# Block 0's products at every third mark, the last gather spread to twelve columns from the end, block 6's outputs divided between the last two phases

## The chip, the core and the metric

The kernel runs on one core of one Trainium2 chip. The metric is the device time of one execution in microseconds (us). Five engines work side by side, each in its own fixed order of instructions: PE (TensorE, matmuls; PEld is its weight load), DVE (VectorE), ACT (ScalarE), POOL (GpSimd, which here issues the gathers) and SP (SyncE, which issues the other transfers). An engine whose next instruction waits lets nothing behind it pass.

## The reference, cut to what matters

Of the 1024 tokens, each picks 8 times 16 experts out of 16384; an expert is one row of 1024 numbers in `u_tab` and one in `v_tab`.

```
def block(xb):                    # 128 tokens
    ...
    idx = jnp.take_along_axis(cand_i, best_pos, axis=-1)      # 128 experts a token
    gate = jax.nn.softmax(best_s, axis=-1)
    u = u_tab[idx]
    v = v_tab[idx]
    act = jax.nn.gelu(jnp.einsum('td,thkd->thk', xb, u).astype(jnp.float32))
    return jnp.einsum('thk,thkd->td', (gate * act).astype(xb.dtype), v)
```

A mixer (norm, pooling, gated part, output projection) stands before this and a norm behind it. The change touches neither.

## The kernel before

The 1024 tokens are eight blocks of 128. The mixer and the scores go over the first 256 tokens, then the middle 512, then the last 256. The expert part is done in two ways.

**Dense, blocks 2 to 5** (the middle 512 tokens). `gates_dense` builds a table of gates with one-hot matmuls (L591, `mm<-oh` and `mu<-oh`, 128 groups of four tokens). Then `dense` goes over 128 columns of 128 experts each: it loads `raw_u` and `raw_v` (512 KB each), splits both into high and low parts (`uh` on ACT, `ul` on DVE, likewise `v`), makes 24 matmuls into `mu`, applies gelu on ACT (L666, `a<-mu`, once a column, so its starts tell where the columns are), multiplies by the gates (L667) and splits the result into `wh` and `wl`. After every third column 72 matmuls into `mm` follow, with eight additions into `hD` on DVE (L645).

**Sparse, blocks 0, 1, 6 and 7.** POOL gathers rows of the tables, one gather for a position j of 128, each 128 rows of 4 KB (512 KB). "U of a block" is 128 gathers from `peer_u`, each followed by one multiply-and-sum on DVE (`sparse_u`, L505, `junk`). "V of a block" follows when its U is whole. For blocks 0, 1 and 6 (`sparse_v`) it is 32 steps; a step is four gathers from `peer_v` and sixteen `po` matmuls on PE (L538). For block 7, the one named by `SUMMED`, it is 128 gathers and 128 multiply-adds on DVE instead, each needing the one before it (`sparse_s`, L559).

The rows land in two sets of buffers: `rowt` with 8 and `rowv` with 4. A gather waits until its buffer's last reader is done. `sparse(phases)` takes phases in turn. `EARLY` runs beside the gates and uses `rowt` alone. `LATE` runs beside the columns. In a phase that has both U and V, U takes `rowv` and V takes `rowt`; in a phase that has one kind alone, gathers go to the two sets by turns, twelve buffers in all. V of block 7 counts as V.

Two things set where a sparse instruction stands. The program's text emits dense columns and sparse steps by turns, at an even pace (the loop at the end of `hybrid_block`), and the framework's scheduler then lays out every engine's order with a clock of its own: of what is ready on that clock it takes what the text has first. A gather that has a free buffer may so come long before its place in the text. `marks` are matmuls of the mixer and gate stage in the order of the text; `anchors` with `BEHIND` say after which mark a step of block 0's V may stand (`behind`, `issue_after`): step j not before mark 4 + 4j.

Of the kernel before, what the change touches and what calls it, by code (L numbers as in the profile page):

```python
# [27 lines left out]
NK = 128  # L28
# [14 lines left out]
GROUP = 3  # L43
# [2 lines left out]
GI = 4  # L46
OH = 3

BEHIND = (4, 4)

TURN = 6

# [1 line left out]
QUAD = 4  # L54

EARLY = ({"U0": 128}, {"U1": 16}, {"V0": 128, "U1": 48})
LATE = ({"U1": 64}, {"V1": 128, "U6": 128}, {"V6": 128, "U7": 128}, {"V7": 128})

SUMMED = 7

RUNS = ((0, 1, 16), (1, 7, 8), (8, 8, 1))
NC = sum(na * nb for _, na, nb in RUNS)
# [3 lines left out]
def hybrid_block(ctx: ExitStack, tc: tile.TileContext, t: dict, out: bass.AP):  # L66
# [399 lines left out]
    def turn(b):  # L466

        d, srcs = picked.pop(b)
        p = ps.tile([P, HALF], F32, name="mm")[:, :P * len(srcs)]
        for i, src in enumerate(srcs):  # L470
            nc.tensor.transpose(p[:, i * P:(i + 1) * P], src, ident)
        nc.vector.tensor_copy(d, p.rearrange("p (i j) -> p i j", j=P))
        turned[b] = d
# [2 lines left out]

    homes = {"U": [(gat, "rowt", ROWS)], "V": [(gat, "rowt", ROWS)]}

    def gather(table, ids, turn):

        home = homes["U" if table == "peer_u" else "V"]
        pool, name, bufs = home[turn % len(home)]
        rowt = pool.tile([P, D], F32, name=name, bufs=bufs)
        ins = nc.gpsimd.indirect_dma_start(out=rowt, out_offset=None, in_=t[table],  # L484
                                           in_offset=bass.IndirectOffsetOnAxis(ap=ids, axis=0))
        return rowt, ins
# [4 lines left out]
    def behind(name, i):  # L491
        at = anchors.get(name, [])
        return tc.issue_after(at[min(i, len(at) - 1)]) if at else None

    def sparse_u(b):

        _, gate, idx = routed[b]
        r2 = r2s[b]
        act = sp.tile([P, P], F32, name="act")
        h = hp.tile([P, D], F32, name="h")  # L500
        nc.sync.dma_start(h, gS[b * P:(b + 1) * P, :])
        for j in range(P):
            r, _ = gather("peer_u", idx[:, j:j + 1], j)
            junk = sp.tile([P, D], BF16, name="junk", bufs=1)
            nc.vector.scalar_tensor_tensor(junk, r, 1.0, h, op0=ALU.mult, op1=ALU.mult, accum_out=act[:, j:j + 1])  # L505
            yield
        w = sp.tile([P, P], F32, name="w", bufs=1)
        nc.scalar.activation(w, act, AF.Gelu_apprx_tanh, scale=r2)
        nc.vector.tensor_mul(w, w, gate)
        if b == SUMMED:  # L510
            routed[b] = w, idx
            return
        pw_ = ps1.tile([P, D], F32, name="wt", tag="po")[:, :P]
        with behind(f"U{b}", 0) or ExitStack():
            nc.tensor.transpose(pw_, w, ident)
        wT = sp.tile([P, P], F32, name="wT")
        nc.vector.tensor_copy(wT, pw_)
        routed[b] = wT

    def sparse_v(b):  # L520
        wT = routed[b]
        idxT = turned[b][:, 0, :]
        po = ps1.tile([P, D], F32, name="po", tag="po")
        wg = wT.rearrange("p (g j) -> p g j", j=32)
        for j in range(32):

            rows_ = []
            for g in range(QUAD):
                rows_.append(gather("peer_v", idxT[:, g * 32 + j:g * 32 + j + 1], j))
                if g < QUAD - 1:  # L530
                    yield
            z = wz[j % len(wz)]
            nc.gpsimd.tensor_copy(z[:, :, 31:32], wg[:, :, j:j + 1])
            with behind(f"V{b}", j) or tc.high_priority():
                first = None
                for g, (r, _) in enumerate(rows_):
                    for q in range(2):
                        mm = nc.tensor.matmul(po[g * 32:(g + 1) * 32, q * HALF:(q + 1) * HALF],  # L538
                                              z[:, g, 31 - j:63 - j], r[:, q * HALF:(q + 1) * HALF],
                                              start=j == 0, stop=j == 31)  # L540
                        first = first or mm
            for _, got in rows_[1:]:
                tc.add_manual_dep(first.ins, got.ins.name,
                                  mybir.DependencyInfo(mybir.DependencyClass.Sync, mybir.DependencyReason.DATA),
                                  reason="four tokens together")
            yield
        y = hp.tile([P, D], F32, name="h")
        nc.sync.dma_start(y, hS[b * P:(b + 1) * P, :])
        nc.vector.tensor_add(y, y, po)
        finish(b, y)  # L550

    def sparse_s(b):

        w, idx = routed[b]
        y = hp.tile([P, D], F32, name="h")
        nc.sync.dma_start(y, hS[b * P:(b + 1) * P, :])
        for j in range(P):
            r, _ = gather("peer_v", idx[:, j:j + 1], j)
            nc.vector.scalar_tensor_tensor(y, r, w[:, j:j + 1], y, op0=ALU.mult, op1=ALU.add)  # L559
            yield  # L560
        finish(b, y)

    def finish(b, y):
        ss = sp.tile([P, 1], F32, name="ss3")
        sq = sp.tile([P, D], BF16, name="junk", bufs=1)
        nc.scalar.activation(sq, y, AF.Square, accum_out=ss)
        r3 = sp.tile([P, 1], F32, name="r3")
        rsqrt(sp, r3, ss, 1.0 / D, 1)
        nc.vector.scalar_tensor_tensor(y, y, r3, fgrow[0], op0=ALU.mult, op1=ALU.mult)
        nc.sync.dma_start(out[b * P:(b + 1) * P, :], y)  # L570
# [116 lines left out]
    def sparse(phases):  # L687


        for phase in phases:  # L690
            n = max(phase.values())
            if beside:
                kinds = {name[0] for name in phase}
                homes["U"] = beside[:1] if len(kinds) > 1 else beside
                homes["V"] = beside[1:] if len(kinds) > 1 else beside
            for i in range(n):
                for name, m in phase.items():
                    unit = QUAD if name[0] == "V" else 1
                    for _ in range(((i + 1) * m // n // unit - i * m // n // unit) * unit):
                        if name not in parts:  # L700
                            b = int(name[1:])
                            parts[name] = [(sparse_u if name[0] == "U" else sparse_s if b == SUMMED else sparse_v)(b), 0]
                        part = parts[name]
                        next(part[0])
                        part[1] += 1
                        if part[1] == P:
                            for _ in part[0]:
                                pass
                        yield
# [92 lines left out]
    steps = 8 + DBLK * P // TB  # L802
# [20 lines left out]
    for b in (6, 7):  # L823
        for _ in pick(tk, b):
            pass
        if b != SUMMED:
            turn(b)
    gps.close()
    rts.close()
    anchors.update({"U0": [marks[1]], "V0": marks[BEHIND[0]::BEHIND[1]]})  # L830
    for _ in sparse(EARLY):
        pass
    gavs = ExitStack()
    gav = opened(gavs, name="gav", bufs=VROWS, reuse_waits="tile")

    beside += [(gav, "rowv", VROWS), (gat, "rowt", ROWS)]
    gathered = sparse(LATE)
    steps = sum(sum(phase.values()) for phase in LATE)
    done = 0
    for c in dense(de, xdh, xdl):  # L840
        while done * (NK - GROUP) < min(c + 1, NK - GROUP) * steps:
            next(gathered, None)
            done += 1
    gavs.close()
# [45 lines left out]
```

## Time and profile before

| | |
|---|---|
| median of 3 executions (lowest, highest) | 2595.39 us (2581.85, 2601.49) |
| the profiled execution, device time | 2595.38 us |
| its span, first to last instruction | 2593.4 us |
| busy: PE, DVE, POOL, ACT | 2366.7, 1996.6, 1301.3, 764.5 us |
| mean granted clock of PE | 0.962 |
| gates with block 0's V, about | 525 to 951 us |
| columns, first and last `a<-mu` | 951.2 and 2542.1 us |

The span holds everything that the rows below speak of; 2.0 us of the device time lie around it. Shares over the whole span mix stages with different limits, so the rows below are of single stretches of the column loop: where U of one block runs beside V of another, where only U or only block 7's V runs, and the end.

### The profile page before, as it was taken

To read this page: it belongs to the slowest core of one execution; us is meant where nothing else is said; L and a number is where in the kernel's file an instruction comes from. 1 tells how busy PE (TensorE), PEld (TensorE's weight loads), DVE (VectorE), ACT (ScalarE), POOL (GpSimd) and SP (SyncE) were. 2 spreads that over 40 slices of the span, in tenths; PEclk is the share of its full clock that TensorE was granted. 3 is DMA by queue.
4 is the path that set the end of the run, shared out by engine and by line. 5 is a ranking of instruction groups with operands and counts; after the bars stand their busy time and mean duration, and the time that the engine had idled before them with its cause. 6 is when DMAs were issued, how large, how long until landed. Compare 5 with 4: busy or idle time off the path is not lost.

```text
span 2593.4 us, 33440 instructions
## 1 busy us (share of the span) xinstructions
PE 2366.7 (91%) x11454; PEld 1842.0 (71%) x11454; DVE 1996.6 (77%) x4376; ACT 764.5 (29%) x1418; POOL 1301.3 (50%) x1195
## 2 busy tenths in 40 slices
PE   7997999889987668999999999999999999999993
PEld 6886788767665446777667777876767678777773
DVE  2289979995888964898575667986666678898898
ACT  2221011136666642222221222222122222222221
POOL 0033754224455662556666655456666663455552
PEclk9998899999999789999999999999999999999997
DMA  6667998859888897999999999989999998898984
GB/s 237 211 238 242 368 385 309 296 182 360 309 315 303 317 345 280 337 361 370 362 390 381 375 363 332 321 316 388 378 370 375 393 379 306 292 327 307 320 283 164
DMA packets 292585, 835.58 MB, mean 322 GB/s; under 512 B 25152, under 2 KB 105536, under 8 KB 290368
## 3 DMA queue, kind: packets, MB, share of 16 engines
q0 software_dynamic: 147456, 536.94, 55.9%
q1 hardware_dynamic: 144960, 296.53, 32.5%
q8 instruction: 90, 1.47, 0.2%
q14 instruction: 79, 0.65, 0.1%
HBM read 787.23 MB, written 46.14 MB: 321 GB/s over the span
## 4 chain that ended last, share of the span: by engine, by line
PE 51%; DVE 24%; DMA 12%; issue 10%; ACT 2%; POOL 1%; SPq 0%; DVEq 0%; another core or an unknown queue 0%; POOLq 0%; ACTq 0%
PE mm L176 8%; PE po L538 6%; DVE junk L505 6%; PE mm L140 6%; PE mu L142 6%; PE mu L140 6%; PE mm L141 5%; PE mm L142 5%; PE mu L141 5%; DMA raw_u<-uT 4%; DMA rowv<-peer_u,idx 3%; DVE oh L582 2%; PE mm L591 1%; DVE h L559 1%; DVE hD L645 1%
## 5 line engine op out<-in xcount | busy, mean ns | idle before, releaser
L484 POOL DMA_INDIRECT rowt<-peer_v,idxT x384 | 474.8, 1237 | 369.4 <-PE po L538 146.4
L484 POOL DMA_INDIRECT rowt<-peer_u,idx x224 | 272.3, 1216 | 438.4 <-DVE top L374 166.1
L484 POOL DMA_INDIRECT rowv<-peer_u,idx x288 | 333.3, 1157 | 292.6 <-DVE junk L505 234.4
L140 PE MATMUL mm<-vh,wh 128*128 128x512 f32 x1024 | 395.6, 399 | 27.7 <-ACT wh L132 24.5
L140 PE MATMUL mu<-xdh,uh 128*128 128x512 f32 x1024 | 402.7, 393 | 15.4 <-ACT uh L132 15.4
L142 PE MATMUL mu<-xdh,ul 128*128 128x512 f32 x1024 | 401.4, 392 | 7.5 <-DVE ul L133 7.5
L141 PE MATMUL mm<-vl,wh 128*128 128x512 f32 x1024 | 401.4, 393 | 1.5 <-DVE vl L133 1.5
L141 PE MATMUL mu<-xdl,uh 128*128 128x512 f32 x1024 | 400.3, 391 | 0.0
L505 DVE SCALAR_TENSOR_TENSOR junk<-rowv,h 128x1024 bf16<-128x1024 f32 x288 | 351.7, 1221 | 49.7 <-DMA rowv<-peer_u,idx 43.7
L142 PE MATMUL mm<-vh,wl 128*128 128x512 f32 x1024 | 369.2, 391 | 0.0
L645 DVE TENSOR_TENSOR hD<-hD,mm 128x512 f32<-128x512 f32 x344 | 226.1, 683 | 95.4 <-PE mm L142 64.4
L505 DVE SCALAR_TENSOR_TENSOR junk<-rowt,h 128x1024 bf16<-128x1024 f32 x224 | 272.3, 1216 | 28.9 <-DMA rowt<-peer_u,idx 27.3
L140 PEld LDWEIGHTS mm<-vh,wh 128*128 128x128 f32 x1024 | 192.9, 189 | 108.7 <-ACT wh L132 36.0
L140 PEld LDWEIGHTS mu<-xdh,uh 128*128 128x128 f32 x1024 | 192.7, 188 | 68.1 <-ACT uh L132 20.5
L142 PEld LDWEIGHTS mu<-xdh,ul 128*128 128x128 f32 x1024 | 192.9, 188 | 57.0 <-DVE ul L133 11.8
L538 PE MATMUL po<-rowt,wz 128*32 128x512 f32 x1536 | 211.2, 628 | 16.8 <-DMA rowt<-peer_v,idxT 16.5
L142 PEld LDWEIGHTS mm<-vh,wl 128*128 128x128 f32 x1024 | 192.0, 188 | 47.8 <-issue 5.9
L141 PEld LDWEIGHTS mm<-vl,wh 128*128 128x128 f32 x1024 | 193.5, 189 | 43.6 <-DVE vl L133 2.4
L141 PEld LDWEIGHTS mu<-xdl,uh 128*128 128x128 f32 x1024 | 193.0, 188 | 41.5 <-issue 1.7
L667 DVE TENSOR_TENSOR a<-a,gc 128x512 f32<-128x512 f32 x128 | 88.1, 689 | 170.1 <-ACT a L666 128.3
L132 ACT ACTIVATE uh<-raw_u 128x1024 fp32r<-128x1024 f32 x128 | 134.9, 1054 | 261.9 <-DMA raw_u<-uT 221.9
L666 ACT ACTIVATE a<-mu 128x512 f32<-128x512 f32 x128 | 75.8, 593 | 461.0 <-PE mu L142 384.3
(163 smaller groups left out, 3588.8 us busy)
## 6 DMA issues: line engine op xcount, KB each, us to landing
raw_u<-uT SPq DMA_DIRECT2D x128, 512.0 KB
raw_v<-peer_v SPq DMA_DIRECT2D x128, 512.0 KB
G<-gs SPq DMA_DIRECT2D x16, 2048.0 KB
gc<-G SPq DMA_DIRECT2D x32, 1024.0 KB
w<-wq SPq DMA_DIRECT2D x48, 512.0 KB
w<-w_in SPq DMA_DIRECT2D x36, 512.0 KB
w<-w_out SPq DMA_DIRECT2D x24, 512.0 KB
h<-x SPq DMA_DIRECT2D x16, 512.0 KB
```

What stands on the lines that cost most here:

```text
L132: nc.scalar.activation(hi, src, AF.Copy)
L140: nc.tensor.matmul(dst, lh, rh, start=first and c == 0, stop=False)
L141: nc.tensor.matmul(dst, lh, rl, start=False, stop=False)
L142: nc.tensor.matmul(dst, ll, rh, start=False, stop=last and c == n - 1)
L176: mm = nc.tensor.matmul(dst[:, i, :], lhs, rhs, start=c == 0, stop=c == NDC - 1)
L484: ins = nc.gpsimd.indirect_dma_start(out=rowt, out_offset=None, in_=t[table], in_offset=bass.IndirectOffsetOnAxis(ap=ids, axis=0))
L505: nc.vector.scalar_tensor_tensor(junk, r, 1.0, h, op0=ALU.mult, op1=ALU.mult, accum_out=act[:, j:j + 1])
L538: mm = nc.tensor.matmul(po[g * 32:(g + 1) * 32, q * HALF:(q + 1) * HALF], z[:, g, 31 - j:63 - j], r[:, q * HALF:(q + 1) * HALF], start=j = ...
L582: nc.vector.tensor_tensor(oh, iota_k[:, None, None, :].to_broadcast([P, 2, TB, NK]), iT[:, 0:2, tok:tok + TB, None].to_broadcast([P, 2, TB ...
L645: nc.vector.tensor_add(hq, hq, p)
L666: nc.scalar.activation(a, p, AF.Gelu_apprx_tanh)
L667: nc.vector.tensor_mul(a.rearrange("i (k t) -> i k t", t=GT), a.rearrange("i (k t) -> i k t", t=GT), gc[:, :, c % GI, :])
```

## The change

Three edits in numbers and one in the choice of buffers. `BEHIND` lets step j of block 0's V stand from mark 2 + 3j on. `AHEAD` paces the text so that the last sparse step is emitted with column 116 rather than 125 (by the old form NK - GROUP). `LATE` gives the third phase half of block 6's V, and the fourth phase the other half beside block 7's V. For that phase block 7's V is counted as U: it takes one gather at a time, and `rowv` alone, while block 6's V has `rowt`.

```
-BEHIND = (4, 4)
+BEHIND = (2, 3)
...
-LATE = ({"U1": 64}, {"V1": 128, "U6": 128}, {"V6": 128, "U7": 128}, {"V7": 128})
+LATE = ({"U1": 64}, {"V1": 128, "U6": 128}, {"V6": 64, "U7": 128}, {"V6": 64, "V7": 128})
...
+AHEAD = 12
...
-    def gather(table, ids, turn):
-        home = homes["U" if table == "peer_u" else "V"]
+    def gather(table, ids, turn, kind):
+        home = homes[kind]
...
-            r, _ = gather("peer_v", idx[:, j:j + 1], j)
+            r, _ = gather("peer_v", idx[:, j:j + 1], j, "U")
...
-                kinds = {name[0] for name in phase}
+                kinds = {"U" if name == f"V{SUMMED}" else name[0] for name in phase}
...
-                    unit = QUAD if name[0] == "V" else 1
+                    unit = QUAD if name[0] == "V" and name != f"V{SUMMED}" else 1
...
-        while done * (NK - GROUP) < min(c + 1, NK - GROUP) * steps:
+        while done * (NK - AHEAD) < min(c + 1, NK - AHEAD) * steps:
```

The gather of block 7's V is the line with `idx`; the other calls of `gather` hand over "U" or "V" as their table had it.

What the scheduler makes of it, at three places. Lines of the changed kernel stand two lower. With the edit of `AHEAD` alone, every engine's order is that of before, row for row; with `BEHIND` alone and with `LATE` and the buffers alone it is not.

First, PE where block 0's V begins (`po` is a step of it; `mm<-x,w` are the mixer's projections). Before:

```order
L515 MATMUL wt<-ident,w 128x128
L355 MATMUL mm<-ks,tmp 128x128 x2
L176 MATMUL mm<-x,w 128x256 x32
L271 MATMUL mm<-d,pw 128x256
L176 MATMUL mm<-x,w 128x256 x15
L271 MATMUL mm<-d,pw 128x256
L176 MATMUL mm<-x,w 128x256
L538 MATMUL po<-rowt,wz_87 32x512 x8
L271 MATMUL mm<-d,pw 128x256
L176 MATMUL mm<-x,w 128x256 x15
L271 MATMUL mm<-d,pw 128x256
L176 MATMUL mm<-x,w 128x256
```

The same place in the changed kernel:

```order
L517 MATMUL wt<-ident,w 128x128
L357 MATMUL mm<-ks,tmp 128x128 x2
L178 MATMUL mm<-x,w 128x256 x32
L540 MATMUL po<-rowt,wz_87 32x512 x8
L273 MATMUL mm<-d,pw 128x256
L178 MATMUL mm<-x,w 128x256 x15
L273 MATMUL mm<-d,pw 128x256
L178 MATMUL mm<-x,w 128x256
L273 MATMUL mm<-d,pw 128x256
L178 MATMUL mm<-x,w 128x256 x16
L540 MATMUL po<-rowt,wz_89 32x512 x8
L273 MATMUL mm<-d,pw 128x256
```

Step 0 moved 16 projections forward, and step 1, which stood behind the first gate matmuls, now stands 32 projections ahead of that place. From there on step j + 1 of the changed kernel stands about where step j stood: it is ahead by one step throughout. When the columns begin, five steps are left rather than six.

Second, POOL from the end of block 6's V on (`rowt<-peer_v,idxT` is block 6's V, `rowv<-peer_u` block 7's U, `peer_v,idx` block 7's V). Before:

```order
L484 DMA rowt<-peer_v,idxT 128x1024 x4
L533 COPY wz_89<-wT 128x4
L484 DMA rowv<-peer_u,idx 128x1024 x2
L484 DMA rowt<-peer_v,idxT 128x1024 x4
L484 DMA rowv<-peer_u,idx 128x1024 x3
L484 DMA rowt<-peer_v,idx 128x1024 x4
L484 DMA rowv<-peer_u,idx 128x1024 x3
L484 DMA rowt<-peer_v,idx 128x1024 x4
L484 DMA rowv<-peer_u,idx 128x1024 x41
L484 DMA rowv<-peer_v,idx 128x1024 x5
L484 DMA rowt<-peer_v,idx 128x1024
L484 DMA rowv<-peer_v,idx 128x1024
```

The last two rows repeat by turns nearly to the end. The same place in the changed kernel, to the end of the program:

```order
L486 DMA rowv<-peer_u,idx 128x1024 x4
L486 DMA rowt<-peer_v,idxT 128x1024 x4
L535 COPY wz_87<-wT 128x4
L486 DMA rowv<-peer_u,idx 128x1024
L486 DMA rowt<-peer_v,idxT 128x1024 x4
L535 COPY wz_89<-wT 128x4
L486 DMA rowv<-peer_u,idx 128x1024 x4
L486 DMA rowt<-peer_v,idxT 128x1024 x4
L486 DMA rowv<-peer_u,idx 128x1024 x53
L486 DMA rowv<-peer_v,idx 128x1024 x128
```

All of block 6's V still stands ahead of the last 53 gathers of block 7's U; none of it stands beside block 7's V. What differs is that all 128 gathers of block 7's V now go to `rowv`.

Third, DVE at the end (`h<-row.` is block 7's V, `hD` the last dense sums). Before:

```order
L559 SCALAR_TENSOR_TENSOR h<-rowt,w,h 128x1024
L645 TENSOR_TENSOR hD_7472<-hD_7472,mm 128x512 x2
L559 SCALAR_TENSOR_TENSOR h<-rowv,w,h 128x1024
L645 TENSOR_TENSOR hD_7473<-hD_7473,mm 128x512 x2
L559 SCALAR_TENSOR_TENSOR h<-rowt,w,h 128x1024
L559 SCALAR_TENSOR_TENSOR h<-rowv,w,h 128x1024
```

Eleven more rows of L559 follow these, thirteen behind the last `hD` in all. In the changed kernel:

```order
L561 SCALAR_TENSOR_TENSOR h<-rowv,w,h 128x1024
L647 TENSOR_TENSOR hD_7472<-hD_7472,mm 128x512 x2
L561 SCALAR_TENSOR_TENSOR h<-rowv,w,h 128x1024
L647 TENSOR_TENSOR hD_7473<-hD_7473,mm 128x512 x2
L561 SCALAR_TENSOR_TENSOR h<-rowv,w,h 128x1024 x7
```

Seven stand behind the last `hD`, six fewer. Those six stand earlier among the columns: DVE's order has 202 instead of 195 of L505 and L559 before the ninth column, 459 instead of 460 before the eighty-ninth, and 494 instead of 488 before the ninety-seventh.

## Rows read from the trace of the kernel before

**Rows 1.** The page's head: the span, and each engine's busy time, share and count.

```profile
span 2593.4 us, 33440 instructions
PE 2366.7 (91%) x11454; PEld 1842.0 (71%) x11454; DVE 1996.6 (77%) x4376; ACT 764.5 (29%) x1418; POOL 1301.3 (50%) x1195
```

**Rows 2.** Busy time by stretch: the stretch and its length, then each engine's busy us and instructions, the granted clock, the DMA share and GB/s. In order: the gates; the first columns; U alone on twelve buffers; U alone on four; V of block 6 beside U of block 7; U alone on four; V of block 7 alone on twelve.

```profile
525.00:951.00 426.00, 344.05 (x2024) 257.38 (x2024) 359.77 (x1019) 256.30 (x696) 216.00 (x172) 0.90 0.83 304
951.00:1060.00 109.00, 91.06 (x429) 68.19 (x428) 56.35 (x84) 28.93 (x38) 41.62 (x40) 0.92 0.85 309
1060.00:1205.00 145.00, 140.92 (x613) 113.86 (x615) 136.21 (x215) 37.76 (x49) 82.65 (x67) 0.99 0.97 354
1574.00:1716.00 142.00, 139.36 (x617) 113.20 (x607) 124.52 (x186) 38.59 (x50) 66.01 (x55) 1.00 0.93 322
1803.00:2080.00 277.00, 274.92 (x1353) 196.18 (x1353) 177.02 (x253) 64.59 (x83) 175.95 (x167) 1.00 1.00 377
2145.00:2250.00 105.00, 99.40 (x427) 80.53 (x426) 90.86 (x138) 30.28 (x40) 40.22 (x36) 0.98 0.88 302
2255.00:2540.00 285.00, 275.74 (x1200) 225.27 (x1199) 259.13 (x275) 75.51 (x99) 152.53 (x108) 0.99 0.87 302
```

**Rows 3.** Line L666, once a column, in the stretches 1060 to 1205, 1574 to 1716, 1803 to 2080, 2145 to 2250 and 2255 to 2540: count, then shortest, median and longest ns, and first and last start.

```profile
L666 ACT ACTIVATE a<-mu x13: 576/598/602, 1069.1 to 1204.6; 128x512 f32<-128x512 f32 x13
L666 ACT ACTIVATE a<-mu x12: 576/580/600, 1591.5 to 1715.9; 128x512 f32<-128x512 f32 x12
L666 ACT ACTIVATE a<-mu x22: 579/598/600, 1802.7 to 2073.6; 128x512 f32<-128x512 f32 x22
L666 ACT ACTIVATE a<-mu x9: 578/598/600, 2144.9 to 2241.6; 128x512 f32<-128x512 f32 x9
L666 ACT ACTIVATE a<-mu x25: 573/581/601, 2254.8 to 2528.5; 128x512 f32<-128x512 f32 x25
```

**Rows 4.** The sparse instructions on DVE, lines L505 and L559, in the stretches 1060 to 1205 (two rows), 1574 to 1716, 2145 to 2250 and 2255 to 2540 (two rows), same columns.

```profile
L505 DVE SCALAR_TENSOR_TENSOR junk<-rowv,h x33: 1212/1219/1226, 1059.5 to 1200.2; 128x1024 bf16<-128x1024 f32 x33
L505 DVE SCALAR_TENSOR_TENSOR junk<-rowt,h x30: 1214/1218/1227, 1061.8 to 1193.5; 128x1024 bf16<-128x1024 f32 x30
...
L505 DVE SCALAR_TENSOR_TENSOR junk<-rowv,h x50: 1211/1219/1254, 1578.8 to 1714.1; 128x1024 bf16<-128x1024 f32 x50
...
L505 DVE SCALAR_TENSOR_TENSOR junk<-rowv,h x37: 1215/1219/1248, 2146.1 to 2248.6; 128x1024 bf16<-128x1024 f32 x37
...
L559 DVE SCALAR_TENSOR_TENSOR h<-rowv,w,h x54: 1272/1279/1286, 2255.6 to 2536.3; 128x1024 f32<-128x1024 f32 x54
L559 DVE SCALAR_TENSOR_TENSOR h<-rowt,w,h x54: 1274/1280/1286, 2258.6 to 2538.4; 128x1024 f32<-128x1024 f32 x54
```

**Rows 5.** DVE's waits, total us, times and longest, in the stretches 1574 to 1716, 2145 to 2250 and 2255 to 2540, the two longest of each.

```profile
DVE junk L505 <- DMA rowv<-peer_u,idx: 8.1, 6, 3.1
DVE ul L133 <- ACT uh L132: 4.4, 5, 2.0
...
DVE junk L505 <- DMA rowv<-peer_u,idx: 6.7, 3, 3.2
DVE ul L133 <- ACT uh L132: 4.2, 5, 1.2
...
DVE ul L133 <- ACT uh L132: 20.9, 12, 3.5
DVE hD L645 <- PE mm L142: 3.8, 10, 1.2
```

**Rows 6.** The chain of work that ended last, cut to 2145 to 2250, its steps that are gathers: start, us, what.

```profile
2175.68 10.87 DMA rowv<-peer_u,idx
...
2213.99 5.37 DMA rowv<-peer_u,idx
...
2222.48 9.23 DMA rowv<-peer_u,idx
```

**Rows 7.** DVE's timeline at the end, start, us, what: the last `hD`, the first and the last of the thirteen L559 behind it, and the first row of the final norm.

```profile
2556.37 1.28 DVE L645 TENSOR_TENSOR hD<-hD,mm 128x512 f32<-128x512 f32 x2
2557.57 1.28 DVE L559 SCALAR_TENSOR_TENSOR h<-rowt,w,h 128x1024 f32<-128x1024 f32 x1
...
2573.41 1.28 DVE L559 SCALAR_TENSOR_TENSOR h<-rowt,w,h 128x1024 f32<-128x1024 f32 x1
2575.91 0.15 DVE L118 TENSOR_SCALAR rs_v<-ss 128x1 f32<-128x1 f32 x1 [1.22 <-ACT junk L566]
```

**Rows 8.** PE's timeline, 500 to 600, line L538: the first three steps of block 0's V.

```profile
524.96 1.95 PE L538 MATMUL po<-rowt,wz 128*32 128x512 f32 x16
567.15 3.27 PE L538 MATMUL po<-rowt,wz 128*32 128x512 f32 x16
575.84 1.94 PE L538 MATMUL po<-rowt,wz 128*32 128x512 f32 x16
```

**Rows 9.** The longest wait of POOL, 500 to 951, and of DVE for a gather, 500 to 940: total us, times, longest.

```profile
POOL rowt L484 <- PE po L538: 135.4, 23, 30.4
...
DVE junk L505 <- DMA rowt<-peer_u,idx: 22.8, 7, 6.1
```

**Rows 10.** Busy time of the instructions on `po` alone, by stretch: PE, PEld and DVE busy us and counts, then clock, DMA share and GB/s.

```profile
1803.00:2080.00 277.00, 42.77 (x352) 10.51 (x352) 0.00 (x0) 1.00 1.00 377
...
2255.00:2540.00 285.00, 0.00 (x0) 0.00 (x0) 0.00 (x0) 0.99 0.87 302
```

More of the change, by code (lines that the diff above doesn't have):

```diff
@@ L502, in sparse_u @@
         for j in range(P):
-            r, _ = gather("peer_u", idx[:, j:j + 1], j)
+            r, _ = gather("peer_u", idx[:, j:j + 1], j, "U")
             junk = sp.tile([P, D], BF16, name="junk", bufs=1)
@@ L528, in sparse_v @@
             for g in range(QUAD):
-                rows_.append(gather("peer_v", idxT[:, g * 32 + j:g * 32 + j + 1], j))
+                rows_.append(gather("peer_v", idxT[:, g * 32 + j:g * 32 + j + 1], j, "V"))
                 if g < QUAD - 1:
```

## The prediction

> **What bounds the kernel now.** I read the page first: PE is busy 91% of the span, DVE 77%, POOL 50% [rows 1]. These are means over stages with different limits, so I cut the column loop where the mix of sparse work changes [rows 2] and took the time of a column from the starts of `a<-mu` [rows 3]. The reader should see two regimes. Where V of block 6 runs beside U of block 7, PE is busy 274.9 of 277 us, DVE only 177.0, and DMA moves 377 GB/s at a share of 1.00 [rows 2]; a column takes (2073.6 - 1802.7) / 21 = 12.90 us [rows 3]. PE and DMA set the pace. Where U or block 7's V runs alone, DVE is busy 136.2 of 145, 124.5 of 142, 90.9 of 105 and 259.1 of 285 us, and DMA is below that peak [rows 2]; DVE sets the pace. Columns there take 11.29 us (1060 to 1205), 11.31 (1574 to 1716), 12.09 (2145 to 2250) and 11.40 (2255 to 2540) [rows 3], with 63, 50, 37 and 108 sparse instructions on DVE [rows 4].
>
> Those four differ in buffers too. With twelve buffers (the first and the last) DVE never waits for a gather long enough to be among its longest waits; with `rowv` alone it waits 8.1 us for 50 gathers and 6.7 us for 37 [rows 4, 5], 0.16 to 0.18 us each.
>
> Before the columns, in the gates, DVE is busy 359.8 of 426 us [rows 2], and POOL stands 135.4 us for a `po` step [rows 9]. In the first columns DVE is busy only 56.4 of 109 us [rows 2].
>
> **The change, part by part.** *The pace of twelve columns.* The order of each engine is the same with and without this edit (see the change). The scheduler's clock, the buffers and the data decide where a gather stands, and the text's pace was not what held it. It costs and brings 0.
>
> *Block 6's V divided.* In POOL's new order all of it still stands ahead of block 7's last U gathers. The gathers of the second half find free `rowt` buffers while U waits for its four `rowv`, and are hoisted out of the fourth phase. PE and DVE are therefore not evened out between the last phases; by itself this brings 0.
>
> *Block 7's V on four buffers.* Here is the cost. Every gather now needs the multiply-add four places ahead of it to be done. 122 of the 128 stand among the columns. Lower bound: 0, as in the stretch now, where DVE has no gather among its waits [rows 5]; nothing in having fewer buffers saves time. Upper bound of the same kind of stretch: 0.18 x 122 = 22 us. I expect part of it to lie in waits that DVE has anyway. It now stands 20.9 us in 285 for `ul<-ACT uh`, which is `raw_u` landing late, but 4.2 us in 105 and 4.4 in 142 on four buffers [rows 5], that is about 10 us in 285. If gathers take the place of 11 us of that, 22 - 11 = 11 us are left. The columns say about the same. At 1.30 us a sparse instruction, (37 / 105) x 12.09 = 4.26 of them a column go with 12.09 us, and the last stretch has (108 / 285) x 11.40 = 4.32 with 11.40: 0.7 us more a column on four buffers. The other stretch has 3.98 with 11.31, or 11.75 at 4.32: 0.35 more. Over the 122 / 4.32 = 28 columns that is 10 to 20 us. I take 12.
>
> What is late next: `vl` and `ul` stand behind the waiting instruction on DVE, and PE's `mu` needs `ul`. Both engines then stand for the same wait, and DVE is the pace there (259.1 of 285 us busy, with 24.7 of its idle time in the two waits shown [rows 2, 5]), so I count it once.
>
> The Trainium skill, DMA: Bandwidth & Descriptors, section Anatomy of one DMA, gives about 2.0 us plus bytes over 436 GB/s for such a transfer, which for 512 KB would be an estimate of 3.2 us. Four buffers would then never be short, the cost would be 0, and the sum below 12 us lower. The trace does not agree: gathers on the chain take 5.4 to 10.9 us [rows 6].
>
> *Six fewer at the end.* Behind the last `hD` DVE now makes thirteen multiply-adds, 2557.57 to 2573.41 + 1.28, 1.32 us apart, and only then can the norm of block 7 and the four outputs follow [rows 7]. The new order has seven there: 6 x 1.32 = 7.9 us less. That they were moved costs nothing only where DVE has room: about seven lie ahead of the ninth column, in the stretch where DVE is busy half the time [rows 2], and most of the rest in the columns where V of block 6 now ends two steps sooner. Bounds: 7.9 us less, or 0, if the seven last gathers come only one in 2.6 us on four buffers (7 x 2.6 = 18 us against 17.2 now). I take 7.9, since the waits are counted above.
>
> *Block 0's V from mark 2 on, every third.* Its first step is on PE at 525.0 us, the second only at 567.2, the third at 575.8 [rows 8], so two steps' buffers stand held for some 42 us. In the new order both stand ahead of that gap, and a lead of one step remains, no more, because gathers and `po` then wait for each other by turns [rows 9]. The spacing of three marks is not what sets the order. The end of the gates hangs on DVE's work, which is the same. Bounds: a loss of about 13 us, if PE, one step earlier each time, waits for a gather (one step of 32 in 426 us); a gain of 22.8 us, if DVE's waits for gathers in that stage all go [rows 9]. The cover in between is DVE's other work, so I take 0 besides the share already in the six.
>
> **Sum.** 2593.4 + 12 - 7.9 = 2597.5 us of span, with the 2.0 us around it 2599.5. The profiled execution took 2595.38 and the median is 2595.39, so nothing has to be shifted: 2599 us, +0.1%.
>
> **The rivals.**
>
> *Slower: the ring of four sets the pace.* A buffer's turn is the gather, POOL's issue of it (40.2 / 36 = 1.1 us [rows 2]) and DVE's 1.28. With 9.2 us as one of the chain's gathers has it [rows 6], a turn is 11.6 us, or 2.90 us a gather, where DVE now uses one in 285 / 108 = 2.64 [rows 4]. Then (2.90 - 2.64) x 122 = 32 us more, and with 10.9 us for the gather (3.31) 82. It decides from a gather of 4 x 2.64 - 2.4 = 8.2 us on. For it: two of the three on the chain are longer. Against it: the two stretches on four buffers show at most 0.18 us of wait a gather, not 0.26, and the chain picks the slow ones. Time: 2593.4 + 32 - 7.9 + 2 = 2620, to 2670.
>
> *Faster: the lead of the first steps goes through.* POOL's longest wait for `po`, 30.4 us [rows 9], has about the length of the gap ahead of the second step [rows 8]; if the gathers, U of block 1 and the columns' start all come that much sooner, and the four buffers cost nothing: 2593.4 - 30.4 - 7.9 + 2 = 2557. For it: DVE waits 22.8 us for those gathers. Against it: DVE is busy 84% of that stage and its work there is no less.
>
> *Faster: the regimes are evened out after all.* [...] In this kernel it would take 16 steps of `po` at 42.77 / 22 = 1.94 us, 31 us, from where PE sets the pace to where there is none now [rows 10], and give 2593.4 - 31 - 7.9 + 2 = 2557. The order speaks against it: no step moved there.
>
> **How the numbers follow.** One per cent, about what a measurement of this kernel can tell from no change, is 26 us. My case, every part small: 0.74, at 2599. Ring of four: 0.13. Lead goes through: 0.10. Evened out: 0.03. The range holds my case with its bounds: down, 2595.4 - 7.9 - 10 = 2577, with no wait and half the gain of the first steps; up, 2595.4 + 22 + 0 = 2617, all of the waits and nothing won at the end. That leaves out the three others and some of my own, about 2 in 10. Faster by over 1% is 0.13, within 1% 0.74, slower 0.13.
>
> **What would show it.** Right: the twelve buffers' stretch of block 7's V shows `h<-rowv` waiting for DMA, 10 to 22 us in all; its columns take 11.7 to 12.1 us; seven multiply-adds close DVE; no `po` beside block 7's V; `po` ends among the same columns as before; the second step of block 0's V comes before 560 us; the first `a<-mu` stays near 951. Wrong: a column there of over 12.5 us (the ring), a first `a<-mu` before 930 (the lead), `po` beside block 7's V (evened out), or a stage that I costed at 0 and that moved by more than 15 us.

## The result and the profile after

| | before | after |
|---|---|---|
| median of 4 executions each (lowest, highest) | 2592.64 us (2581.85, 2601.49) | 2626.14 us (2611.88, 2633.03) |
| ratio, 95% interval | | 1.012 (1.0082 to 1.0158) |
| span of the profiled execution | 2593.4 us | 2618.7 us (device time 2621.12) |

The change makes the kernel slower by 1.2%, and the time lies above the predicted range. The page's head, against [rows 1]: the same work, with PE busy 17 us more.

```profile
span 2618.7 us, 33439 instructions
PE 2383.9 (91%) x11454; PEld 1851.4 (71%) x11454; DVE 1996.7 (76%) x4376; ACT 763.6 (29%) x1418; POOL 1300.7 (50%) x1195
```

To find where the 25.3 us of span arise, I cut both traces at the same columns, by the starts of `a<-mu`, counted from column 0 (all in us):

| stretch | before | after | difference |
|---|---|---|---|
| start to column 0 | 951.2 | 942.8 | -8.4 |
| column 0 to 15 | 185.1 | 177.4 | -7.7 |
| 15 to 48 | 436.8 | 448.5 | +11.7 |
| 48 to 72 | 301.1 | 317.5 | +16.4 |
| 72 to 102 | 380.6 | 380.7 | +0.1 |
| 102 to 126 (block 7's V) | 273.7 | 293.1 | +19.4 |
| 126 to the end | 64.9 | 58.7 | -6.2 |
| sum | 2593.4 | 2618.7 | +25.3 |

Two stretches lose, and the first of them, columns 15 to 72, is one in which neither the buffers nor the divided phase have a part. The windows of columns 15 to 48, 48 to 72, 72 to 102 and 102 to 126, after (busy us and counts of PE, PEld, DVE, ACT, POOL, then granted clock, DMA share, GB/s):

```profile
1120.20:1568.70 448.50, 437.27 (x2106) 313.89 (x2105) 297.92 (x429) 104.47 (x133) 284.61 (x263) 0.99 0.97 364
1568.70:1886.20 317.50, 300.77 (x1378) 225.32 (x1378) 224.31 (x337) 76.78 (x99) 169.52 (x154) 0.97 0.92 332
1886.20:2266.90 380.70, 371.71 (x1734) 279.37 (x1733) 278.09 (x400) 98.10 (x125) 197.99 (x179) 0.99 0.93 337
2266.90:2560.00 293.10, 272.43 (x1153) 222.06 (x1153) 252.61 (x274) 73.29 (x97) 139.90 (x104) 0.96 0.85 291
```

The same columns before:

```profile
1136.30:1573.10 436.80, 428.71 (x2085) 308.54 (x2087) 294.16 (x424) 105.06 (x134) 272.57 (x257) 1.00 0.99 372
1573.10:1874.20 301.10, 293.66 (x1374) 223.69 (x1373) 230.99 (x350) 76.44 (x100) 172.77 (x153) 1.00 0.95 345
1874.20:2254.80 380.60, 373.65 (x1765) 279.26 (x1764) 275.19 (x408) 98.12 (x126) 211.37 (x194) 1.00 0.97 358
2254.80:2528.50 273.70, 264.44 (x1151) 215.88 (x1150) 249.09 (x264) 73.36 (x97) 146.82 (x102) 0.99 0.88 305
```

In the second row the counts of PE hardly differ (1378 and 1374) and DVE does less, yet PE stands 16.7 us instead of 7.4, is busy 7.1 us longer for the same matmuls, and has a granted clock of 0.97 instead of 1.00. Over both rows PE stands 12.4 us longer and is busy 15.7 us longer, with 25 matmuls more; by the clock records of the traces its granted clock is at the lower of its two levels (1.2 GHz of 2.4) for 27.3 us of these columns after, and never before. No engine has become the bound: DMA moves less too. The engines wait for each other more. PE's waits in columns 15 to 72 (total us, times, longest), after:

```profile
PE mm L142 <- ACT wh L134: 11.5, 8, 2.2
PE mu L142 <- ACT uh L134: 6.7, 4, 2.6
PE po L540 <- DMA rowt<-peer_v,idxT: 4.1, 1, 4.1
PE mu L144 <- DVE ul L135: 3.2, 4, 1.3
```

and before:

```profile
PE mu L142 <- DVE ul L133: 4.5, 6, 1.2
PE mm L140 <- ACT wh L132: 4.1, 8, 1.2
PE mu L140 <- ACT uh L132: 3.0, 4, 1.6
...
PE po L538 <- DMA rowt<-peer_v,idxT: 1.4, 1, 1.4
```

One such place shows what a wait costs. PE's timeline after (start, us, what, and in brackets the idle time and what ended it):

```profile
1744.02 0.39 PE L144 MATMUL mm<-vh,wl 128*128 128x512 f32 x1
1748.50 3.67 PE L540 MATMUL po<-rowt,wz 128*32 128x512 f32 x16 [4.09 <-DMA rowt<-peer_v,idxT]
1752.10 0.80 PE L144 MATMUL mm<-vh,wl 128*128 128x512 f32 x1
1752.69 0.63 PE L142 MATMUL mm<-vh,wh 128*128 128x512 f32 x1
1753.12 0.43 PE L143 MATMUL mm<-vl,wh 128*128 128x512 f32 x1
```

PE stands 4.09 us for a gather of block 1's V, and the sixteen `po` matmuls behind the wait take 3.67 us, where a step took 1.95 and 1.94 in [rows 8]; the next dense matmul takes 0.80 us instead of 0.39. The granted clock has fallen to its lower level (1.2 GHz), so a part of the wait is paid again, about 2.3 us here: 1.7 us in the `po` matmuls and some 0.6 us in the dense ones behind them. The window around this place has a mean granted clock of 0.89.

```profile
1735.00:1765.00 30.00, 24.59 (x114) 16.59 (x113) 16.02 (x24) 4.41 (x6) 24.56 (x23) 0.89 1.00 388
```

The Trainium skill, TensorE: Matmul & The Clock Gate, section HAM oscillation, describes a kernel in which a wait for a DMA between matmuls lowers the clock, so that the matmuls behind it start slow. These rows agree.

Why was the gather late? POOL's timeline after:

```profile
1720.96 1.70 POOL L486 DMA_INDIRECT rowv<-peer_u,idx  x1 [6.33 <-DVE junk L507]
1723.84 1.80 POOL L486 DMA_INDIRECT rowv<-peer_u,idx  x1 [1.18 <-DVE junk L507]
...
1739.22 1.50 POOL L486 DMA_INDIRECT rowt<-peer_v,idxT  x1 [0.30 <-issue]
```

The last gather of the step is issued at 1739.22 and lands some 9 us later. It stands in POOL's order behind two gathers of U that waited 6.33 and 1.18 us for a `rowv` buffer, that is for DVE. About the same columns before, the step waits 1.42 us only and then runs at full pace:

```profile
1752.10 1.95 PE L538 MATMUL po<-rowt,wz 128*32 128x512 f32 x16 [1.42 <-DMA rowt<-peer_v,idxT]
```

POOL's wait alone is not the difference, for before it waits as long ahead of this step (POOL's timeline before; the second line is the step's last gather):

```profile
1730.50 1.75 POOL L484 DMA_INDIRECT rowv<-peer_u,idx  x1 [6.16 <-DVE rs_a L123]
...
1743.48 0.94 POOL L484 DMA_INDIRECT rowt<-peer_v,idxT  x1 [0.30 <-PE mm L142]
```

What differs is how soon PE comes to the step. Before, it comes 7.2 us after the step's last gather is issued (1752.10 - 1.42 - 1743.48), and in the changed kernel 5.2 us after (1748.50 - 4.09 - 1739.22); the wait ends over 8 us after the issue in both.

### The profile page after: what moved, and what is told of

Read it like the earlier page. It is cut to its first block, busy times and chain, and to the rows that moved or that the text cites. A ratio compares the mean times of both kernels' runs of the same rounds, so it can differ in the third digit from the quotient of the medians.

```text
span 2618.7 us, 33439 instructions
## 1 busy us (share of the span) xinstructions
PE 2383.9 (91%) x11454; PEld 1851.4 (71%) x11454; DVE 1996.7 (76%) x4376; ACT 763.6 (29%) x1418; POOL 1300.7 (50%) x1195
## 4 chain that ended last, share of the span: by engine, by line
PE 41%; DMA 13%; DVE 9%; issue 8%; POOL 3%; ACT 2%; POOLq 0%; SPq 0%; DVEq 0%; ACTq 0%
PE mm L142 6%; PE mm L143 5%; PE mu L142 5%; PE po L540 5%; PE mu L144 5%; PE mm L144 5%; PE mu L143 5%; DMA rowv<-peer_u,idx 4%; DMA raw_u<-uT 3%; POOL rowv L486 3%; DMA rowv<-peer_v,idx 2%; DVE junk L507 2%; PE mm L178 2%; DVE oh L584 2%; PE mu L593 1%
## 5 line engine op out<-in xcount | busy, mean ns | idle before, releaser
L486 POOL DMA_INDIRECT rowt<-peer_v,idxT x384 | 469.1, 1222 | 394.9 <-PE po L540 201.0
L486 POOL DMA_INDIRECT rowv<-peer_u,idx x288 | 342.3, 1189 | 297.4 <-DVE junk L507 237.9
L486 POOL DMA_INDIRECT rowv<-peer_v,idx x128 | 171.1, 1337 | 183.8 <-DVE h L561 154.0
```

## The experiments

Every kernel below is the one before with the edit that is shown, unless it is called the changed one. All but the changed one were timed in five rounds beside the kernel before; n is the number of executions.

| kernel | edit | ratio | 95% interval | n | columns reordered | first `a<-mu` | PE busy in 1136 to 2120 |
|---|---|---|---|---|---|---|---|
| before | | 1 | | | 0 | 951.2 | 967.1 |
| after | all four | 1.012 | 1.0082 to 1.0158 | 4 | 101 | 942.8 | 953.8 |
| e_ahead | AHEAD alone | 1.0003 | 0.9982 to 1.0023 | 12 | 0 | 950.0 | 966.1 |
| e_behind | BEHIND (2, 3) alone | 1.0152 | 1.0118 to 1.0187 | 6 | 111 | 948.6 | 943.9 |
| e_split | LATE and buffers alone | 1.0004 | 0.9983 to 1.0025 | 12 | 22 | 944.1 | 961.9 |
| e_twelve | after, block 7's V on both sets | 1.0094 | 1.0063 to 1.0125 | 6 | 116 | 948.2 | 948.6 |
| n_4_3 | BEHIND (4, 3) | 0.9997 | 0.9973 to 1.0021 | 12 | 14 | 936.5 | 965.6 |
| n_2_4 | BEHIND (2, 4) | 1.0078 | 1.0051 to 1.0105 | 10 | 111 | 940.2 | 956.8 |
| n_4_2 | BEHIND (4, 2) | 1.0026 | 1.0008 to 1.0044 | 12 | 105 | 945.6 | 969.4 |
| n_6_4 | BEHIND (6, 4) | 1.0148 | 1.0113 to 1.0182 | 6 | 114 | 936.9 | 953.2 |
| z_seventeen | one gather moved in the text | 1.0177 | 1.0139 to 1.0215 | 6 | 97 | 938.9 | 951.1 |
| z_twelve | four gathers moved in the text | 1.0011 | 0.999 to 1.0032 | 12 | 110 | 926.5 | 952.5 |
| z_swap | two names swapped | 1.0034 | 1.0014 to 1.0054 | 12 | 52 | 939.6 | 960.4 |
| c_split | after, with BEHIND (4, 3) | 1.0007 | 0.999 to 1.0025 | 12 | 36 | 936.7 | 966.7 |

"Columns reordered" counts those of the 128 in which PE's order of instructions, from the column's first `mu` matmul to the next column's, is not that of before. The table's main result is in it: the four kernels with up to 36 such columns read 0.9997 to 1.0007, `z_swap` with 52 reads 1.0034, and the eight with 97 and more, three of which share `BEHIND` (2, 3), lie anywhere from 1.0011 to 1.0177.

**Which part costs.** The first theory (A) put the loss down to `BEHIND` and the order in the middle that it brings; its rival (B) to block 7's V on four buffers.

```
e_ahead:  +AHEAD = 12, and NK - AHEAD for NK - GROUP at the pace
e_behind: -BEHIND = (4, 4)
          +BEHIND = (2, 3)
e_split:  the diff with BEHIND = (4, 4) and AHEAD = 3 (the old pace)
```

> Before with the pace of twelve columns alone: every engine's order is that of before. Both theories expect 1.000 and an interval that holds 1; how far the columns' starts of its trace lie from those of before (951.2, 1573.1, 1874.2, 2254.8, 2528.5 us) tells how much two traces of one order differ by themselves. If they differ by 10 us or more in a stage, nothing of that size may be read from one trace.

> Before with BEHIND = (2, 3) alone; block 7's V keeps twelve buffers. Theory A (the new order of the middle columns, which BEHIND alone sets off, costs most: in the trace of the changed kernel columns 48 to 72 took 16 us more than before) expects +12 to +20 us, 1.005 to 1.008, with the gap open by column 90. Theory B (the four buffers of block 7's V alone cost it all) expects -8 to +3 us, 0.997 to 1.001.

> Before with block 6's V divided in the text and block 7's V on rowv alone, BEHIND as before; the orders up to column 88 are those of before. Theory A expects +8 to +14 us (1.003 to 1.005): 17 to 19 us more from column 102 to 126, 5 less behind the last column. Theory B expects all of it, +25 to +33 us (1.010 to 1.013).

The pace is worth nothing, as its equal order had said. The trace of `e_ahead`, with the order of before, also tells how far two traces of one order differ: by up to 3.1 us in a stretch of the first table and 4.6 us at a column's start, so differences of that size are not read below. `BEHIND` alone costs 1.5%, no less than the whole change and two to three times what A expected; `LATE` and the buffers together cost nothing in time (1.0004, where A expected 1.003 to 1.005; columns 102 to 126 took 5.2 us more, where it expected 17 to 19). Theory B falls; A had the place right, but the size too small for `BEHIND` and too large for the other two. Beside `BEHIND` the other edits seem to take back some 0.3% (1.0152 to 1.012), which neither expected; the intervals overlap, so this is not shown.

What makes `BEHIND`'s order dear is seen best where it returns: up to column 88 `e_behind` has the order of after. Its PE stands at the same place, longer still:

```profile
1757.49 0.39 PE L142 MATMUL mm<-vh,wl 128*128 128x512 f32 x1
1763.84 3.66 PE L538 MATMUL po<-rowt,wz 128*32 128x512 f32 x16 [5.96 <-DMA rowt<-peer_v,idxT]
1767.43 0.80 PE L142 MATMUL mm<-vh,wl 128*128 128x512 f32 x1
```

In columns 15 to 90 after has fourteen places at which the starts of two matmuls lie over 1.3 us apart. Ten of them return in `e_behind` in the same column at the same pair of instructions (columns 31, 44, 50, 53, 58, 61, 62, 66, 70 and 82; in the last three with the same 1.71, 2.46 and 2.46 us). Before has five, the longest 2.1 us, and only two of them in one of these ten columns. `e_twelve` below, with PE's order of after up to column 74, has ten of the fourteen too. So the gaps belong to the order for the greater part, though not one by one: of the five of before, two return in `e_ahead`.

**Twelve buffers for block 7's V.** The changed kernel, with block 7's gathers going to both sets by turns:

```
-            r, _ = gather("peer_v", idx[:, j:j + 1], j, "U")
+            r, _ = gather("peer_v", idx[:, j:j + 1], j, "S")
...
+                homes["S"] = beside
```

> The changed kernel, but block 7's V gathers by turns into both sets, twelve buffers, as before. Since it now shares rowt with block 6's V, half of the latter does stand beside block 7's V in the order, to the end. Theory A expects the middle to stay dear: 1.004 to 1.010 before any gain at the end. Theory B expects 1.000 or less. If evening out the two regimes is worth the 31 us that the prediction's third rival gave it, 0.99 to 0.995; if po to the very end lengthens the tail by 8 us or more, that shows behind the last column.

1.0094 is within what A expected, but the run does not measure the buffers alone: now that block 7's V takes `rowt` as well, a part of block 6's V does stand beside it, twelve of its 32 steps (192 matmuls). The window of columns 102 to 126, `po` alone (PE and PEld busy us and counts, then DVE):

```profile
2264.80:2582.40 317.60, 23.33 (x192) 5.73 (x192) 1.22 (x1) 0.95 0.87 318
```

So it is a test of the evening out of regimes instead. The Trainium skill, Perfetto Trace Analysis, section Optimization Strategy, says that interleaving regimes in which different engines are the most contended may improve performance. Against `e_behind`, columns 72 to 90 take 215.2 us instead of 243.3, columns 102 to 126 take 317.5 instead of 283.9, and what follows column 126 takes 37.2 instead of 61.1. The 28.1 us won in columns 72 to 90 are more than given back in columns 102 to 126 (33.6); what is left of the gain is the shorter tail (23.9). In time the kernel cannot be told from after. Here the columns won less than they lost; as the edit dealt the order anew as well, the run does not show how much of either is the interleaving's own.

**Lead, mark or order.** Four theories of why `BEHIND` costs were set against each other with its neighbours: the closer spacing (D), the early start itself (E), a greater lead of the sparse work over the columns (F), and a re-dealt order as such, whatever made it so (C).

```
n_4_3: BEHIND = (4, 3)     n_2_4: BEHIND = (2, 4)
n_4_2: BEHIND = (4, 2)     n_6_4: BEHIND = (6, 4)
```

> BEHIND = (4, 3) alone, the rest as before: only the spacing of the new pair. The order changes within the gates and is that of before in the columns. Theory C (a re-dealt order of the columns is what costs, whatever mark it came from): ratio 0.998 to 1.002. Theory D (the closer spacing itself, V of block 0 ahead of other work in the gates, costs): 1.006 to 1.015. Theory E (luck of order has nothing to do with it, V beginning at mark 2 does): 0.998 to 1.002.

> BEHIND = (2, 4) alone, the rest as before: only the earlier start of the new pair, with the old spacing. All five orders differ from before through the columns, but about as many sparse steps stand ahead of each column as before (195 or 196 ahead of the ninth, where (2, 3) has 202). Theory C (any re-dealt order of the columns costs or brings some tens of us, by chance): anything from 0.99 to 1.02, and DVE's wait for mm in the stretch of columns 15 to 90 away from 46 us by more than 15. Theory E (the early start costs): 1.012 to 1.018. Theory F (a greater lead of the sparse work in the columns costs): 0.998 to 1.003.

> BEHIND = (4, 2) alone, the rest as before: old start, spacing of two marks, so that the sparse work has 205 steps ahead of the ninth column (before 195, (2, 3) 202). Theory C: anything from 0.99 to 1.02. Theory E (the early start costs): 0.998 to 1.003. Theory F (the lead costs): 1.015 to 1.025, more than (2, 3), with DVE's wait for mm in columns 15 to 90 over 87 us.

> BEHIND = (6, 4) alone, the rest as before: V of block 0 starts two marks later, so that the sparse work lags (fewer steps ahead of each column, 603 to 609 ahead of column 126 where before has 615). Theory C: anything from 0.99 to 1.02. Theory E: 0.998 to 1.003. Theory F (a lead costs, so a lag does not): 0.995 to 1.003, apart from some 8 us more of multiply-adds behind the last column, and DVE's wait for mm in columns 15 to 90 at or under 46 us.

The spacing costs nothing: D falls. The greatest lead that was run, (4, 2), costs 0.3% where F expected 1.5 to 2.5%: F falls. The late start, (6, 4), where E expected nothing and F some 8 us at the end, costs as much as (2, 3) (12.4 us of it behind column 126), and the early start alone half of it, where E expected all: E falls. Time follows neither number. `n_4_3` is the one that leaves the order alone from column 24 on, and the one that costs nothing. Only C is left, but it had allowed anything between 0.99 and 1.02, so it still had to be shown by an edit that has nothing to do with block 0's V.

One reading fell here too. After the first runs I took DVE's wait for `mm` for the mark of the loss: in 1136 to 2120 it is 46.0 us before, 93.2 in after, 87.1 in `e_behind`. In `n_4_2` it is 90.7, and that trace's columns lose nothing: at column 90 it is 1.6 us ahead of before (it is of the fastest execution of `n_4_2`, 2591.92 us against a median of 2600.14). DVE has room there; what counts is whether PE stands and its clock falls. Columns 15 to 126 take 1392.2 us both before and in `n_4_2`, with the granted clock at its lower level for 6.8 and 23.9 us; they take 1439.8 in after and 1451.1 in `e_behind`, with 58.0 us at that level in each. The windows of 1136 to 2120, before:

```profile
1136.00:2120.00 984.00, 967.13 (x4664) 706.74 (x4663) 686.00 (x1003) 240.15 (x306) 604.38 (x558) 1.00 0.98 366
```

and of `n_4_2`:

```profile
1136.00:2120.00 984.00, 969.41 (x4655) 707.38 (x4654) 668.33 (x971) 240.14 (x306) 578.11 (x543) 0.99 0.97 360
```

**Edits that should be worth nothing.** A gather of block 1's U, or four, change places in the text with steps of block 0's V; or two names in a phase are swapped. (H: only the marks of block 0's V cost.)

```
-EARLY = ({"U0": 128}, {"U1": 16}, {"V0": 128, "U1": 48})
+EARLY = ({"U0": 128}, {"U1": 17}, {"V0": 128, "U1": 47})    z_seventeen
+EARLY = ({"U0": 128}, {"U1": 12}, {"V0": 128, "U1": 52})    z_twelve
-..., {"V1": 128, "U6": 128}, ...
+..., {"U6": 128, "V1": 128}, ...                            z_swap
```

> An edit that should be worth nothing: in the text one of block 1's 128 gathers of U moves from the third phase of the early work to the second (17 and 47 in place of 16 and 48); BEHIND, the buffers and the later phases are those of before. The order of all engines still changes from block 0's V to the end of the columns. Theory C (an order of the columns dealt anew costs or brings some tens of us by chance, whatever made it so): a ratio between 0.995 and 1.02 that differs from 1.000 by more than 0.003 in at least one of this kernel and the next; PE's idle time in 1136 to 2120 over 20 us where it is slower. Theory H (only the marks of block 0's V cost): 0.998 to 1.002.

> A second edit that should be worth nothing, of the same kind: 12 and 52 in place of 16 and 48. Theory C: a ratio between 0.995 and 1.02, at least one of this kernel and the last away from 1.000 by more than 0.003. Theory H: 0.998 to 1.002.

> A third edit that should be worth nothing: in the second phase of the late work block 6's U stands ahead of block 1's V in the text instead of behind it. The orders are those of before to the middle of the columns, differ for a part of that phase, and SP's order differs in two rows only. Theory C by the size of what is dealt anew: 0.995 to 1.006, nearer to 1.000 than the two kernels before. Theory H: 0.998 to 1.002.

One gather of 1024, moved from one phase to the one before, costs 1.8%, the most in the table, though its interval overlaps those of (2, 3) and (6, 4). Four cost nothing that can be told. H falls, and C's distinctive claim held. `z_swap` lies in C's range, but not nearer to 1 than both others, as was expected of the smaller re-deal: `z_twelve` is nearer. In `z_seventeen` PE stands most for `uh`, and long at a time (1136 to 2120):

```profile
PE mu L140 <- ACT uh L132: 24.7, 6, 9.3
```

Its trace loses 24.4 us by column 126, and another 17.5 us at the end, since 27 multiply-adds of block 7 stand behind the last `hD` where before has thirteen [rows 7]: that number is dealt anew as well. `z_twelve` has as little PE time in 1136 to 2120 as after and lost 26 us over columns 0 to 90, but its columns began 24.7 us sooner, so PE's busy time alone does not rank the kernels. (That trace is of its slowest execution, 2605.98 us against a median of 2599.59.)

**The change without its costly number.** The changed kernel with the mark and spacing that by themselves leave the order of before from column 24 on (`n_4_3`):

```
-BEHIND = (2, 3)
+BEHIND = (4, 3)
```

> The changed kernel with BEHIND = (4, 3) in place of (2, 3): AHEAD, the divided phase and the four buffers stay. If the loss of the change is that of the columns' order that (2, 3) brings, and the other parts are worth 0.000 as measured: 0.997 to 1.004. If the marks 2 + 3j are not what costs, but their meeting with the divided phase: 1.008 to 1.016.

1.0007: with one number put back the loss of the whole change is gone. It also sets the divided phase and the four buffers by themselves. In columns 102 to 126 `c_split` takes 282.5 us where `n_4_3` takes 277.3, and `e_split` 278.9 where before takes 273.7: 5.2 us each time, not much over the 3.1 us by which two traces of one order differ. DVE's waits in that stretch of `c_split`:

```profile
DVE h L561 <- DMA rowv<-peer_v,idx: 16.4, 10, 3.5
DVE ul L135 <- ACT uh L134: 13.4, 9, 3.1
```

No version beat the kernel before: the best ratios are 0.9997 and 1.0003.

## Why the prediction was wrong, point by point

**The step that failed** is the one on block 0's V: "The spacing of three marks is not what sets the order. The end of the gates hangs on DVE's work, which is the same. [...] so I take 0". I looked for its price in the gates alone, and there it is a gain: the second step comes at 531.33 as predicted (the view is PE's timeline, against [rows 8]),

```profile
510.79 1.94 PE L540 MATMUL po<-rowt,wz 128*32 128x512 f32 x16
531.33 1.94 PE L540 MATMUL po<-rowt,wz 128*32 128x512 f32 x16
566.38 3.09 PE L540 MATMUL po<-rowt,wz 128*32 128x512 f32 x16
```

the first `a<-mu` 8.4 us sooner, and the first fifteen columns another 7.7. But the edit dealt PE's order anew in 101 of the 128 columns (111 with `BEHIND` alone). The front of this document says that the order is not that of before, and I gave that no price. It costs 28.1 us in columns 15 to 72 of after, and by itself 1.5% (about 39 us). The prediction's own sign of being wrong came true there: columns 48 to 72, a stage that I costed at 0, moved by 16.4 us. None of my three rivals was this one. The time fell into the range of the rival on the ring of four (2620 to 2670), but by luck and for another reason: `c_split` has that ring and loses nothing.

**Block 7's V on four buffers**, taken at +12: the mechanism was right, the term too large by itself. The multiply-adds wait for gathers 10.3 us in after (10 to 22 foreseen), 12.8 in `e_split` and 16.4 in `c_split`, and in the last two the wait for `uh` shrinks, as assumed, from 20.9 to 14.0 and from 22.2 to 13.4. Net, that is about 5 us. In after it does not shrink:

```profile
DVE ul L135 <- ACT uh L134: 21.5, 15, 4.1
DVE h L561 <- DMA rowv<-peer_v,idx: 10.3, 8, 3.1
DVE hD L647 <- PE mm L144: 6.9, 6, 3.2
```

and the columns take (2560.0 - 2266.9) / 24 = 12.2 us, just over the 11.7 to 12.1 foreseen:

```profile
L668 ACT ACTIVATE a<-mu x25: 572/581/601, 2266.9 to 2560.0; 128x512 f32<-128x512 f32 x25
```

Of the 19.4 us, 10.2 come without the ring (`e_behind`: 283.9 us there), and 9.2 with it, the divided phase and the pace.

**Six fewer at the end**, -7.9: right, but for the waits that I had as its lower bound. DVE's timeline, against [rows 7]:

```profile
2587.89 1.28 DVE L647 TENSOR_TENSOR hD<-hD,mm 128x512 f32<-128x512 f32 x2
2589.09 5.24 DVE L561 SCALAR_TENSOR_TENSOR h<-rowv,w,h 128x1024 f32<-128x1024 f32 x4
2596.07 1.28 DVE L561 SCALAR_TENSOR_TENSOR h<-rowv,w,h 128x1024 f32<-128x1024 f32 x1 [1.74 <-DMA rowv<-peer_v,idx]
2598.03 1.28 DVE L561 SCALAR_TENSOR_TENSOR h<-rowv,w,h 128x1024 f32<-128x1024 f32 x1 [0.68 <-DMA rowv<-peer_v,idx]
2599.67 1.28 DVE L561 SCALAR_TENSOR_TENSOR h<-rowv,w,h 128x1024 f32<-128x1024 f32 x1 [0.35 <-DMA rowv<-peer_v,idx]
```

Seven, and the last three wait 2.8 us for their gathers: -7.9 + 2.8 = -5.1, and the stretch behind column 126 is 6.2 us shorter.

**The pace and the divided phase**, both 0: right. `e_ahead` reads 1.0003, and no `po` stands beside block 7's V in after.

**The lead goes through**: the gain was there, 16.1 us at column 15, and was lost further on. It seems to be lost without a dearer order too: `n_4_3`, whose order is that of before from column 24 on, is 10.1 us ahead at column 48, 3.3 at column 72 and 1.3 behind at column 126. But `e_ahead`, with the order of before throughout, loses 8.1 us from column 48 to 126 as well, so this is not shown.

**What stays open**: what it is in an order that makes it dear. The runs show that the order decides, that the same order has most of its gaps at the same instructions, and what one gap costs. They do not show how to tell a dear order from a cheap one before it runs; the lead, the mark and DVE's waits for `mm` did not tell it. Nor is it shown whether the 9.2 us are the ring's or the new order's, wholly or in part.

## What to carry to other kernels

Where a scheduler lays out the engines, an edit has two prices: that of the place it touches, and that of the order it deals anew for all that follows; look in the order for how far the difference reaches, and if it reaches to the end, widen the range by what edits worth nothing do (here ratios of 1.001 to 1.018). Do not credit or blame a number for its meaning until a neighbour or an idle edit of the same reach has been timed beside it: (2, 3), (6, 4) and one moved gather cost the same within their intervals. In this kernel such deals are not even-handed: none of the eight with 97 and more reordered columns was faster than the order that it replaced. That this is because the kernel had been tuned is a guess that no run here tests.

## What the runs showed of the hardware that was not expected

A stand of PE can cost about half as much again behind it as it lasted. After 4.09 us of idle time sixteen `po` matmuls took 3.67 us, after 5.96 us they took 3.66, against 1.95 behind a wait of 1.42 us, and the dense matmuls that follow are slow as well (0.80 and 0.63 us against 0.39): 2.3 us behind the first of these waits, and 1.7 us in the `po` alone behind the second.
